# Row statistics of four tiles split between ScalarE and VectorE, an earlier weight column, convolutions queued later, and TensorE's first stage bound to its written sequence

## The chip, the core and the metric

The kernel runs on one core of a Trainium2 chip, as one launch. The metric is device time in microseconds (us) from the start to the end of the program. The profile comes from one further execution; its own time stands beside its span below.

## The reference, cut to what matters

One layer of a hybrid model works on 2048 latent rows of width 1024 (x) and 256 context rows (ctx).

```python
hc = modulate(rmsnorm(ctx, norm_mix), csh1, csc1)
logf_f, k_f, logf_b, k_b, vc = hgrn2_gates(hc @ w_in[:, :3 * w], ...)   # context: final scan states only
h = modulate(rmsnorm(x, norm_mix), sh1, sc1)
o, _, _ = token_mixers(h @ w_in, ..., hf_c, hb_c, ...)                  # 2 scans (4 heads) + gMLP unit (4 heads)
x = x + g1 * (o @ w_out)
h2 = modulate(rmsnorm(x, norm_ffn), sh2, sc2)
a, g = split(h2 @ w_up)                                                 # 2 x 2816 columns
x = x + g2 * ((a * gelu(conv3x3(g) + conv_b)) @ w_down)
return rmsnorm(x, norm_final)
```

`rmsnorm` divides a row by the root of the mean of its squares (plus a small constant). `token_mixers` runs a gated recurrence in both directions over 4 heads of 128 channels, started from the context's final states, and a gated unit that mixes positions in chunks of 128. `conv3x3` is a depthwise convolution over the 32 x 64 grid of latent rows. Everything is float32.

## The kernel before, in words

**Precision and TensorE.** A float32 product is made of three reduced-precision ones: each operand is split into a high part (a cast on ScalarE) and a low part (raw minus high, a subtraction on VectorE or GpSimd), and `mm3` issues high x high, high x low and low x high. All matmuls and transposes go through the class `Tensor` (L56 to L74), which also counts a planned time `t`. Profile rows name L70 for every matmul and L74 for every transpose, so products are told apart by their tiles: `pj` (input projection), `sc` and `mi` (scan, transposes), `dn` and `up` (later stages).

**Stage 1, the input projection and the scan (L183 to L1194).** x is done in two halves of 1024 rows, each transposed and modulated into `xh` and `xl` (8 blocks of 128 channels by 1024 rows). `run_banks` (L536) takes a list of banks: a column of 128 output channels and 512 rows (256 for context), so 24 matmuls a bank, followed by a sink that hands the result on. Before a bank it makes sure that the weights of this column and the next exist: `load_raw` (L209) issues a load on SP's queue, `split_w` (L216) casts on ScalarE and subtracts on VectorE, late for the next column in the steady state (there is then one raw buffer). Between the eighths of a 512-row bank `slot()` gives side work its turn: three pumps (`Pump`, L134) hold generators that write out a few instructions, then name the planned time after which they want the next turn. `need` (L647) steps a pump until something is done.

**Order.** `pin` (`keep_in_program_order`) puts an instruction behind the one traced before it on its engine. The program may move the others, by its own estimate of when operands are ready. Here the transposes of x in `x_first` (L414) and `x_second` (L451) are pinned, the other matmuls and transposes of the stage are not.

**Start of x.** Four tiles `xg` (L350) and then four tiles `xk` (L427) of 128 rows make the first half of x. `x_square` (L244) squares a tile on ScalarE with the row sum as a second output, `x_scale` (L249) makes the reciprocal root through `rstd` (L115, GpSimd) and scales the tiles on VectorE. `x_start` (L426) writes this out among the context's banks; the first bank of x needs `xg` transposed ("x0a"), the second needs `xk` ("x0b"). Their written order is the list in L1144, where `c` is a context bank. `ctx_state` (L618) makes a context head's states; `add_ctx(0)` is called ahead of the first bank of x.

**The second half of x.** It is prepared by `x_second`, parked in DRAM and loaded again after the first sequence of banks (L1150 to L1153: 16 loads, 8 for the first 512 rows, 8 for the rest). The second sequence (L1155) begins with the columns 0 and HW of the gate; the first run is told to prepare column 0 ahead (`peek`, L539), column HW is loaded by the second run. The scan of a head is `hg` (L783). The first half's reverse direction waits for states of the second and is finished by `deferred` (L887), whose results go through `o_out` (L742): squares on ScalarE, `rstd`, scaling to `on` on VectorE, and then transposes of `on` on TensorE, each a callback some planned us after the last. Ahead of the last four banks `wo_hook` calls `open_wo` (L1158), which steps all pumps until they are empty, so that buffers can be given over to the output projection.

**Output projection (L1353 to L1388).** 16 row tiles, each 48 matmuls into `dn`, then add x, square, and after each pair `second_norm` (L1295), which transposes and modulates for the next stage. For the last pair its first yield is 9.0. `fetch_x` (L1344) loads x's rows; the last tile shares a buffer with the weights of unit 1, the second of the units of the next stage, so that unit's second half loads only behind the eviction.

**Up-projection and convolution (L1586 to L1619).** A unit (L1231) makes 256 columns with seven products of 12 matmuls in place of eight (a Strassen scheme), for each half of the rows. `prep` (L1247) splits operands three products ahead: cast to `Ah` on ScalarE, subtraction to `Al` on GpSimd. After a gate unit's last product `after` (L1505) appends two convolutions to `work`; each (`conv`, L1431) is a first step on ScalarE and 8 taps on VectorE over 128 x 1024, then a Gelu on ScalarE. Two convolution steps are written out after each product. In the second half (`hh` = 1) the one grid row that straddles the halves (`edges`) gets three small taps on VectorE (L1444), its Gelu (L1459) and its product on GpSimd (L1460). `need` (L1478) steps convolutions until a result exists. Then comes the down-projection.

Of the kernel before, what the change touches and what calls it, by code (L numbers as in the profile page):

```python
# [18 lines left out]
P = 128  # L19
D = 1024  # L20
# [35 lines left out]
class Tensor:  # L56


    def __init__(self, engine):
        self.engine, self.t = engine, 0.0  # L60

    def matmul(self, out, lhsT, rhs, **kw):
        n = 1
        for _, count in rhs.ap[1:]:
            n *= count
        if lhsT.ap[1][1] < P and out.ap[0][1] == lhsT.ap[1][1]:
            self.t += 2 * (n / 1200 + 0.016) / 4
        else:
            self.t += n / 2400 + 0.0135 if rhs.dtype == F32R else 2 * max(0.112, n / 1200 + 0.005)
        return self.engine.matmul(out, lhsT, rhs, **kw)  # L70

    def transpose(self, out, in_, identity):
        self.t += 0.109
        return self.engine.transpose(out, in_, identity)  # L74
# [3 lines left out]
def tile_trunk(ctx, tc, x, c, cx, c_ctx, w_ada, b_ada, norm_mix, norm_ffn, w_in, hg_norm, sgu_g, sgu_b,  # L78
# [105 lines left out]
    with es1:  # L184
# [59 lines left out]
        def x_square(xs, ss, i0=0, keep=pin):  # L244
            for i, xt in enumerate(xs):
                jk = pm.tile([P, D], BF16, tag="acc", name="xjk")
                keep(S.activation(jk, xt, AF.Square, accum_out=ss[:, i0 + i:i0 + i + 1]))

        def x_scale(xs, ss, keep=pin):  # L249

            r = rstd(pm, ss[:, :len(xs)], len(xs), 1.0 / D, keep=keep)
            for i, xt in enumerate(xs):
                keep(V.tensor_scalar(out=xt, in0=xt, scalar1=r[:, i:i + 1], scalar2=None, op0=ALU.mult))
# [100 lines left out]
        with tc.manual_schedule():  # L354
# [55 lines left out]
            x_square(xg[:2], xss, keep=lambda i: i)  # L410
# [3 lines left out]
        def x_first(g0, xs):  # L414
            for k in range(NK):
                pt = bank("mi")
                for i in range(4):
                    pin(T.transpose(pt[:, i * P:(i + 1) * P], xs[i][:, k * P:(k + 1) * P], ident))
                sl = slice(g0 * P, g0 * P + 512)
                x_mod(pt, k, xh[:, k, sl], xl[:, k, sl], 512, S if k % 2 else V)  # L420
                if k % 2:
                    yield 1.6
# [3 lines left out]
        def x_start():  # L426
            xs = [key_tile(t, name="xk") for t in "MMMR"]  # L427
            ss = x_sums()
            x_square(xg[2:], ss)
            yield 1.0  # L430
# [105 lines left out]
        def run_banks(banks, peek=None):  # L536

            keys = [(b[0], b[2]) for b in banks]
            tail = [(peek, 512)] if peek is not None else []  # L539
            for i, (col, n0, n, sink, pre) in enumerate(banks):  # L540
# [4 lines left out]
                for key in up[:2]:  # L545
                    if key not in nxt:
                        nxt[key] = split_w(key, raws["w"] == [0] and key != up[0])
# [7 lines left out]
                for k in range(k0, NK):  # L555
                    if k and n == 512:
                        slot()
                        if k == 3:
                            split_low()
                        if k == 6 and len(up) > 2 and up[2] not in nxt and not w_raw:  # L560
                            load_raw(up[2])
                    w_products(pj[:, :n], (hi, lo), hiT, loT, sl, k, k + 1)
# [115 lines left out]
        ctx_banks = banks  # L678

# [459 lines left out]
        xa = [(xa[0][0], 0, 512, xa[0][3], lambda p=xa[0][4]: (need(bg_q, "x0a"), add_ctx(0), p())),  # L1139
# [9 lines left out]
        run_banks(seq, 0)  # L1149
        for q in range(0, TH, 512):  # L1150
            for k in range(0, NK, 2):
                ld(xh[:, k:k + 2, q:q + 512].bitcast(F32), xh_d[:, k:k + 2, q:q + 512])
                ld(xl[:, k:k + 2, q:q + 512].bitcast(F32), xl_d[:, k:k + 2, q:q + 512])  # L1153
# [40 lines left out]
        hg_q.flush()  # L1194

# [98 lines left out]
    with tc.tile_pool(name="po", bufs=1, reuse_waits="tile") as po:  # L1294
# [49 lines left out]
        def fetch_x(t):  # L1344
            xt = raw_tile2(2 if t == nt_ - 1 else 1 + 2 * (t % 2))
            ld(xt.rearrange("p a b -> p (a b)"), x[t * P:(t + 1) * P, :])
            return xt.rearrange("p a b -> p (a b)")
# [5 lines left out]
        for t, (hh, g) in enumerate(tiles):  # L1353
# [4 lines left out]
            if t + 1 < nt_:  # L1358
                ops[t + 1] = split_o(t + 1, raw_o.pop(t + 1))
                xts[t + 1] = fetch_x(t + 1)  # L1360
            if t + 2 == nt_:
                units[0].load()
            if t + 1 == nt_:
                units[1].load_half(0)
# [14 lines left out]
            if t + 1 == nt_:  # L1379
                units[1].load_half(1)  # L1380
            xs.append(xn)
            if g % 2:
                bg_q.drain()
                how = (ubank, 6.0, 3.0) if t + 1 < nt_ else (lambda: dbank()[:, 0, :], 9.0, 4.5)
# [35 lines left out]
    vals, work, tapped = {}, [], set()  # L1420
# [10 lines left out]
    def conv(hh, f, e):  # L1431
# [6 lines left out]
        for t in range(1, 9):  # L1438
            V.scalar_tensor_tensor(out=cr, in0=gt[:, t // 3:t // 3 + RH, t % 3:t % 3 + GW],  # L1439
                                   scalar=taps[:, t * NF + f:t * NF + f + 1], in1=cr, op0=ALU.mult, op1=ALU.add)  # L1440
            yield
        if hh:
            for t in range(6, 9):
                V.scalar_tensor_tensor(out=e[:, 0, :], in0=gt[:, 1, t % 3:t % 3 + GW],  # L1444
                                       scalar=taps[:, t * NF + f:t * NF + f + 1], in1=e[:, 0, :],
                                       op0=ALU.mult, op1=ALU.add)
# [10 lines left out]
        else:  # L1457
            pin(S.activation(vt[:, GW:], cp, AF.Gelu))
            S.activation(e[:, 0, :], e[:, 0, :], AF.Gelu)  # L1459
# [18 lines left out]
    def need(which, key):  # L1478

        while key not in which:  # L1480
            if not conv_step():
# [23 lines left out]
    def after(u, i, p):  # L1505
# [32 lines left out]
        if kind == "g" and i == 6:  # L1538
            for ff in (f, f + 1):
# [4 lines left out]
                work.append(conv(hh, ff, edge(hh, ff)))  # L1544
# [41 lines left out]
    for n, (u, i) in enumerate(prods):  # L1586
# [32 lines left out]
        conv_step() and conv_step()  # L1619
    assert not work  # L1620
# [250 lines left out]
```

## Time and profile before

| | |
|---|---|
| median of 3 runs | 2398.88 us (2397.96 to 2399.17) |
| profiled execution, its own time | 2401.17 us |
| its span in the trace | 2399.4 us |
| mean granted clock of TensorE | 0.995 |
| busy share: TensorE, VectorE, ScalarE, GpSimd | 98%, 71%, 41%, 33% |

Times in the trace count from the start of the span. A row of the timeline gives the start, the duration, the engine (PE is TensorE, DVE VectorE, ACT ScalarE, POOL GpSimd, SPq SP's queue of transfers), the line, and what is written from what; in brackets how long the engine had stood and what released it. Matmuls overlap in the pipeline, so their durations are longer than the distance of their starts. The granted clock (PEclk) is a share of TensorE's 2.4 GHz.

### The profile page before, as it was taken

How to read it: one execution, taken by the hardware profiler on the slowest of the kernel's cores; microseconds unless marked ns; L12 is line 12 of the kernel's file. 1: busy time of each engine (PE TensorE's matmuls, PEld its weight loads, DVE VectorE, ACT ScalarE, POOL GpSimd, SP SyncE). 2: the span in 40 equal slices, each digit the busy share in tenths (PEclk: the TensorE clock that was granted, in tenths of full speed). 3: DMA queues.
4: the chain of work that ended last, by engine and by line, in shares of the span. 5: the costliest groups of instructions: out<-in, count | busy, mean ns of one | idle time of the engine just before them, and what ended most of it. 6: DMA issues, size and time to landing. Idle time of an engine off the chain costs nothing.

```text
span 2399.4 us, 38721 instructions
## 1 busy us (share of the span) xinstructions
PE 2347.6 (98%) x14951; PEld 1935.9 (81%) x14951; DVE 1701.9 (71%) x2331; ACT 977.9 (41%) x1762; POOL 799.7 (33%) x741
## 2 busy tenths in 40 slices
PE   7999999999999999999999999999999999999998
PEld 5787887878887887887788888888788888888887
DVE  4655677556667653666898787689999984776876
ACT  4673443443445442544433333334333333232343
POOL 0010000000211111003787877878787860000011
PEclk9999999999999999999999999999999999999999
DMA  8454443574435536678522223642222259844744
GB/s 308 150 184 148 135 125 120 184 276 152 160 120 180 177 115 220 205 242 290 180 90 88 83 92 94 248 166 87 87 93 88 85 176 342 270 145 134 250 154 168
DMA packets 305428, 396.39 MB, mean 165 GB/s; under 512 B 33609, under 2 KB 216657, under 8 KB 302557
## 3 DMA queue, kind: packets, MB, share of 16 engines
q1 hardware_dynamic: 301956, 393.17, 49.4%
q8 instruction: 118, 1.93, 0.3%
q10 hardware_dynamic: 3289, 0.76, 0.1%
q14 instruction: 65, 0.53, 0.1%
HBM read 284.73 MB, written 109.13 MB: 164 GB/s over the span
## 4 chain that ended last, share of the span: by engine, by line
PE 50%; POOL 1%; DVE 1%; DMA 1%; issue 0%; SPq 0%; ACT 0%; POOLq 0%; ACTq 0%
PE up L70 32%; PE dn L70 17%; POOL Al L126 1%; DMA raw<-in_w_up_dram 0%; POOL raw L1265 0%; POOL cv L1534 0%; POOL fl L1261 0%; DMA m<-cv 0%; DVE dn L1439 0%; DMA sT<-wd 0%; DVE fl L126 0%; DVE fl L1314 0%; DMA gs<-gp 0%; SPq L1541 0%; DVE gp L1523 0%
## 5 line engine op out<-in xcount | busy, mean ns | idle before, releaser
L1439 DVE SCALAR_TENSOR_TENSOR dn<-gp,taps,dn 128x1024 f32<-128x1024 f32 x352 | 449.0, 1282 | 14.7 <-ACT dn L1436 11.6
L70 PE MATMUL up<-yfar,Ah 128*128 128x512 f32 x1232 | 394.5, 390 | 0.0
L70 PE MATMUL dn<-thl,mhl 128*128 128x512 f32 x1680 | 381.0, 389 | 0.0
L126 POOL TENSOR_TENSOR Al<-raw,Ah 128x512 fp32r<-128x512 f32 x264 | 343.9, 1314 | 79.0 <-ACT Ah L125 76.9
L70 PE MATMUL pj<-xh,whi 128*128 128x512 f32 x896 | 368.4, 411 | 0.0
L70 PEld LDWEIGHTS dn<-thl,mhl 128*128 128x128 f32 x1680 | 315.5, 188 | 65.4 <-issue 0.2
L70 PE MATMUL pj<-xh,wlo 128*128 128x512 f32 x896 | 351.1, 392 | 1.1 <-DVE wlo L225 1.1
L70 PE MATMUL pj<-xl,whi 128*128 128x512 f32 x896 | 350.8, 392 | 0.3 <-DVE xl L126 0.3
L125 ACT CAST Ah<-raw 128x512 fp32r<-128x512 f32 x264 | 162.4, 619 | 317.9 <-PE up L70 254.4
L70 PE MATMUL up<-xah,Al 128*128 128x512 f32 x704 | 275.5, 391 | 5.6 <-POOL Al L126 5.5
L70 PE MATMUL up<-xah,Ah 128*128 128x512 f32 x704 | 275.3, 391 | 1.2 <-ACT Ah L125 1.2
L70 PEld LDWEIGHTS up<-yfar,Ah 128*128 128x128 f32 x1232 | 231.6, 188 | 48.0
L70 PE MATMUL up<-xal,Ah 128*128 128x512 f32 x528 | 205.7, 390 | 0.0
L70 PE MATMUL up<-yfar,Al 128*128 128x512 f32 x528 | 205.5, 389 | 0.0
L70 PEld LDWEIGHTS pj<-xh,wlo 128*128 128x128 f32 x896 | 168.5, 188 | 38.4 <-DVE wlo L225 1.8
L70 PEld LDWEIGHTS pj<-xh,whi 128*128 128x128 f32 x896 | 169.1, 189 | 35.3 <-issue 3.5
L70 PEld LDWEIGHTS pj<-xl,whi 128*128 128x128 f32 x896 | 169.2, 189 | 29.1 <-DVE xl L126 0.6
L70 PE MATMUL dn<-wo,o 128*128 128x512 f32 x768 | 182.8, 394 | 0.8 <-DVE nt L732 0.8
L70 PEld LDWEIGHTS dn<-wo,o 128*128 128x128 f32 x768 | 142.1, 188 | 30.0 <-DVE nt L732 1.0
L70 PEld LDWEIGHTS up<-xah,Al 128*128 128x128 f32 x704 | 132.6, 188 | 35.0 <-POOL Al L126 7.6
L70 PEld LDWEIGHTS up<-xah,Ah 128*128 128x128 f32 x704 | 132.6, 188 | 29.2 <-ACT Ah L125 1.8
L222 ACT CAST whi<-raw 128x1024 fp32r<-128x1024 f32 x68 | 71.3, 1049 | 125.5 <-PE pj L70 102.2
(321 smaller groups left out, 3630.4 us busy)
## 6 DMA issues: line engine op xcount, KB each, us to landing
raw<-in_w_up_dram SPq DMA_DIRECT2D x88, 512.0 KB, 3.7
mr<-m SPq DMA_DIRECT2D x85, 512.0 KB, 5.1
raw<-in_w_in_dram SPq DMA_DIRECT2D x68, 512.0 KB, 4.1
sT<-wd SPq DMA_DIRECT2D x88, 256.0 KB, 4.9
raw<-in_w_ada_dram SPq DMA_DIRECT2D x32, 512.0 KB, 4.9
yfar<-yd SPq DMA_DIRECT2D x14, 1024.0 KB, 17.4
m<-cv SPq DMA_DIRECT2D x22, 544.0 KB, 2.8
raw<-in_w_down_dram SPq DMA_DIRECT2D x22, 512.0 KB, 4.1
```

Source lines behind the costliest of these rows:

```text
L70: return self.engine.matmul(out, lhsT, rhs, **kw)
L125: keep(S.copy(hi, raw))
L126: (eng or G).tensor_sub(lo, raw, hi.bitcast(F32))
L222: S.copy(hi, raw)
L1439: V.scalar_tensor_tensor(out=cr, in0=gt[:, t // 3:t // 3 + RH, t % 3:t % 3 + GW], scalar=taps[:, t * NF + f:t * NF + f + 1], in1=cr, op0=A ...
```

## The change

It has these parts, in the order of the diff:

- `Tensor` has a hook `keep` through which every matmul and transpose goes. From the first `run_banks` of stage 1 to the end of the stage it is `pin`, so TensorE runs the written sequence there.
- Rows of `xg[1]` and `xg[2]` get their mean square on VectorE (`x_stats`: two statistics calls over 512 columns, one that joins them, and two small GpSimd operations for mean squared plus variance) in place of a square on ScalarE. The remaining squares scale by 1/sqrt(1024) so that sums are means.
- `x_start` and `x_first` have other yields, context banks get one more `slot()` in their middle, and `ctx_state` of head 0 is queued one bank earlier.
- Column HW is loaded for the second sequence behind the first 8 loads of x's second half and ahead of the other 8, which are pinned. `peek` becomes a list, and a column in it is not split late.
- The last row tile of x gets a buffer of its own, so unit 1 is loaded whole at the last row tile; the last `second_norm` yields 10.5 first.
- New convolutions go to `fresh` and join `work` at the end of a product, behind that product's casts and steps.
- In the second half the edge's taps are written after tap 4 and its Gelu after tap 6, pinned, in place of after tap 8.

The diff, with the lines of the kernel before at each place:

```diff
@@ L59 @@
     def __init__(self, engine):
-        self.engine, self.t = engine, 0.0
+        self.engine, self.t, self.keep = engine, 0.0, lambda i: i
@@ L69 @@
             self.t += n / 2400 + 0.0135 if rhs.dtype == F32R else 2 * max(0.112, n / 1200 + 0.005)
-        return self.engine.matmul(out, lhsT, rhs, **kw)
+        return self.keep(self.engine.matmul(out, lhsT, rhs, **kw))
@@ L73 @@
         self.t += 0.109
-        return self.engine.transpose(out, in_, identity)
+        return self.keep(self.engine.transpose(out, in_, identity))
@@ L246 @@
                 jk = pm.tile([P, D], BF16, tag="acc", name="xjk")
-                keep(S.activation(jk, xt, AF.Square, accum_out=ss[:, i0 + i:i0 + i + 1]))
+                keep(S.activation(jk, xt, AF.Square, scale=D ** -0.5, accum_out=ss[:, i0 + i:i0 + i + 1]))
+
+        def x_stats(xt, s_, keep=pin):
+            bs = pm.tile([P, 4, 6], F32, tag="bs", name="xbs", bufs=2)
+            mv = pm.tile([P, 4, 2], F32, tag="mv", name="xmv", bufs=2)
+            for i in range(2):
+                keep(V.bn_stats(out=bs[:, i, :], in_=xt[:, i * 512:(i + 1) * 512]))
+            keep(V.bn_aggr(out=mv[:, 0, :], in_=bs[:, :2, :]))
+            keep(G.tensor_mul(s_, mv[:, 0, 0:1], mv[:, 0, 0:1]))
+            keep(G.tensor_add(s_, s_, mv[:, 0, 1:2]))
@@ L251 @@
-            r = rstd(pm, ss[:, :len(xs)], len(xs), 1.0 / D, keep=keep)
+            r = rstd(pm, ss[:, :len(xs)], len(xs), 1.0, keep=keep)
@@ L409 @@
             xss = x_sums()
-            x_square(xg[:2], xss, keep=lambda i: i)
+            x_square(xg[:1], xss, keep=lambda i: i)
+            x_stats(xg[1], xss[:, 1:2], keep=lambda i: i)
@@ L421 @@
                 if k % 2:
-                    yield 1.6
+                    yield 1.3
@@ L428 @@
             ss = x_sums()
-            x_square(xg[2:], ss)
-            yield 1.0
+            yield 0.0
+            yield 0.0
+            x_square(xg[3:], ss, 1)
+            x_stats(xg[2], ss[:, 0:1])
+            yield 2.0
@@ L536 @@
-        def run_banks(banks, peek=None):
+        def run_banks(banks, peek=()):
@@ L538 @@
             keys = [(b[0], b[2]) for b in banks]
-            tail = [(peek, 512)] if peek is not None else []
+            tail = [(col, 512) for col in peek]
@@ L546 @@
                     if key not in nxt:
-                        nxt[key] = split_w(key, raws["w"] == [0] and key != up[0])
+                        nxt[key] = split_w(key, raws["w"] == [0] and key != up[0] and key not in tail)
@@ L555 @@
                 for k in range(k0, NK):
+                    if k and (n == 512 or k == 4):
+                        slot()
                     if k and n == 512:
-                        slot()
@@ L678 @@
         ctx_banks = banks
+        ctx_banks[5] = (*banks[5][:4], lambda: add_ctx(0))
@@ L1138 @@
         xa = part(0, "g0")
-        xa = [(xa[0][0], 0, 512, xa[0][3], lambda p=xa[0][4]: (need(bg_q, "x0a"), add_ctx(0), p())),
+        xa = [(xa[0][0], 0, 512, xa[0][3], lambda p=xa[0][4]: (need(bg_q, "x0a"), p())),
@@ L1148 @@
         seq += rest
-        run_banks(seq, 0)
+        T.keep = pin
+        run_banks(seq, [0])
         for q in range(0, TH, 512):
+            if q:
+                load_raw((HW, 512))
             for k in range(0, NK, 2):
-                ld(xh[:, k:k + 2, q:q + 512].bitcast(F32), xh_d[:, k:k + 2, q:q + 512])
-                ld(xl[:, k:k + 2, q:q + 512].bitcast(F32), xl_d[:, k:k + 2, q:q + 512])
+                for t, d in ((xh, xh_d), (xl, xl_d)):
+                    i = ld(t[:, k:k + 2, q:q + 512].bitcast(F32), d[:, k:k + 2, q:q + 512])
+                    if q:
+                        pin(i)
@@ L1194 @@
         hg_q.flush()
+        T.keep = lambda i: i
@@ L1344 @@
         def fetch_x(t):
-            xt = raw_tile2(2 if t == nt_ - 1 else 1 + 2 * (t % 2))
-            ld(xt.rearrange("p a b -> p (a b)"), x[t * P:(t + 1) * P, :])
-            return xt.rearrange("p a b -> p (a b)")
+            if t == nt_ - 1:
+                xt = first_o[0]()[:, 0].bitcast(F32)
+            else:
+                xt = raw_tile2(1 + 2 * (t % 2))
+            xt = xt.rearrange("p a b -> p (a b)")
+            ld(xt, x[t * P:(t + 1) * P, :])
+            return xt
@@ L1359 @@
                 ops[t + 1] = split_o(t + 1, raw_o.pop(t + 1))
+            if t + 1 < nt_ - 1:
                 xts[t + 1] = fetch_x(t + 1)
+            elif t + 1 == nt_:
+                xts[t] = fetch_x(t)
@@ L1363 @@
             if t + 1 == nt_:
-                units[1].load_half(0)
+                units[1].load()
@@ L1378 @@
             S.activation(pd.rearrange("p a b -> p (a b)"), xn, AF.Square, accum_out=ss[:, g % 2:g % 2 + 1])
-            if t + 1 == nt_:
-                units[1].load_half(1)
@@ L1383 @@
                 bg_q.drain()
-                how = (ubank, 6.0, 3.0) if t + 1 < nt_ else (lambda: dbank()[:, 0, :], 9.0, 4.5)
+                how = (ubank, 6.0, 3.0) if t + 1 < nt_ else (lambda: dbank()[:, 0, :], 10.5, 4.5)
@@ L1420 @@
-    vals, work, tapped = {}, [], set()
+    vals, work, fresh, tapped = {}, [], [], set()
@@ L1440 @@
                                    scalar=taps[:, t * NF + f:t * NF + f + 1], in1=cr, op0=ALU.mult, op1=ALU.add)
+            if hh and t == 4:
+                for tt in range(6, 9):
+                    V.scalar_tensor_tensor(out=e[:, 0, :], in0=gt[:, 1, tt % 3:tt % 3 + GW],
+                                           scalar=taps[:, tt * NF + f:tt * NF + f + 1], in1=e[:, 0, :],
+                                           op0=ALU.mult, op1=ALU.add)
+            if hh and t == 6:
+                pin(S.activation(e[:, 0, :], e[:, 0, :], AF.Gelu))
             yield
-        if hh:
-            for t in range(6, 9):
-                V.scalar_tensor_tensor(out=e[:, 0, :], in0=gt[:, 1, t % 3:t % 3 + GW],
-                                       scalar=taps[:, t * NF + f:t * NF + f + 1], in1=e[:, 0, :],
-                                       op0=ALU.mult, op1=ALU.add)
@@ L1458 @@
             pin(S.activation(vt[:, GW:], cp, AF.Gelu))
-            S.activation(e[:, 0, :], e[:, 0, :], AF.Gelu)
@@ L1480 @@
         while key not in which:
+            if not work:
+                work.extend(fresh)
+                fresh.clear()
@@ L1543 @@
                     ld(gp[ff % 4][:, 0, 1:GW + 1], gs_d[ff][:, 0, :])
-                work.append(conv(hh, ff, edge(hh, ff)))
+                fresh.append(conv(hh, ff, edge(hh, ff)))
@@ L1619 @@
         conv_step() and conv_step()
+        work.extend(fresh)
+        fresh.clear()
```

## Rows read from the trace of the kernel before

**Rows 1.** The page's first part: busy us, share of the span and instructions of each engine.

```profile
PE 2347.6 (98%) x14951; PEld 1935.9 (81%) x14951; DVE 1701.9 (71%) x2331; ACT 977.9 (41%) x1762; POOL 799.7 (33%) x741
```

**Rows 2.** TensorE's waits by releaser, whole span: us in total, times, longest.

```profile
PE up L70 <- POOL Al L126: 5.5, 4, 3.0
...
PE mi L74 <- DVE on L752: 3.1, 3, 1.1
```

**Rows 3.** Timelines of TensorE and ScalarE at the start: start us, us, instruction, [idle before].

```profile
43.42 0.39 PE L70 MATMUL pj<-ch,whi 128*128 128x256 f32 x1 [2.08 <-ACT whi L222]
...
49.11 0.37 ACT L607 COPY vv<-pj 128x256 f32<-128x256 f32 x1 [3.21 <-PE pj L70]
...
64.92 1.07 ACT L247 ACTIVATE xjk<-xk 128x1024 bf16<-128x1024 f32 x1
```

**Rows 4.** VectorE's groups by shape: count, busy us, mean ns, idle before.

```profile
L715 DVE BATCH_NORM_STATS2 bs<-mi 128x6 f32<-128x128 f32 x64 | 16.3, 277 | 13.0 <-PE mi L74 12.9
```

**Rows 5.** Timelines of VectorE and TensorE, 69 to 74 us.

```profile
69.46 2.74 DVE L253 TENSOR_SCALAR xk<-xk,rs 128x1024 f32<-128x1024 f32 x4
...
70.42 0.27 PE L74 MATMUL mi<-ident,xk 128*128 128x128 f32 x1
```

**Rows 6.** Timeline of TensorE, 498 to 508 us.

```profile
498.00 0.40 PE L70 MATMUL pj<-xh,wlo 128*128 128x512 f32 x1
500.58 1.10 PE L70 MATMUL sc<-Q,K 128*32 128x64 f32 x64 [2.18 <-DVE Q L525]
503.72 3.65 PE L74 MATMUL mi<-ident,K 128*128 128x128 f32 x16 [2.04 <-DVE K L595]
```

**Rows 7.** SP's queue, its loads at L1153, VectorE and ScalarE, 487 to 511 us.

```profile
494.10 0.91 SPq L211 DMA_DIRECT2D raw<-in_w_in_dram  x1
...
DMA to landing us min/median/max: 6.3/8.4/10.6
...
487.65 1.22 DVE L225 TENSOR_TENSOR wlo<-raw,whi 128x1024 fp32r<-128x1024 f32 x1
...
509.59 1.05 ACT L222 CAST whi<-raw 128x1024 fp32r<-128x1024 f32 x1
```

**Rows 8.** Windows: stretch, busy us of each engine (instructions), PEclk, DMA share, GB/s.

```profile
503.00:510.00 7.00, 6.28 (x31) 6.31 (x32) 1.62 (x4) 3.89 (x8) 0.00 (x0) 0.52 0.57 196
900.00:914.00 14.00, 11.76 (x63) 9.58 (x63) 4.89 (x7) 4.59 (x19) 4.23 (x5) 1.00 0.52 163
1714.00:1722.00 8.00, 4.98 (x16) 3.73 (x15) 6.18 (x9) 4.00 (x6) 8.00 (x8) 0.79 0.21 79
```

**Rows 9.** Timeline of TensorE, 901 to 914 us.

```profile
901.55 0.48 PE L70 MATMUL pj<-xh,whi 128*128 128x512 f32 x1
...
905.73 0.39 PE L70 MATMUL pj<-xh,whi 128*128 128x512 f32 x1
907.23 0.63 PE L74 MATMUL mi<-ident,on 128*128 128x128 f32 x4 [1.11 <-DVE on L752]
...
908.50 0.47 PE L70 MATMUL pj<-xl,whi 128*128 128x512 f32 x1
...
911.58 0.39 PE L70 MATMUL pj<-xh,wlo 128*128 128x512 f32 x1
913.10 0.63 PE L74 MATMUL mi<-ident,on 128*128 128x128 f32 x4 [1.13 <-DVE on L752]
```

**Rows 10.** Timelines of TensorE and ScalarE, 1132 to 1168 us.

```profile
1133.01 0.55 PE L74 MATMUL dn<-ident,cv 128*128 128x128 f32 x3 [1.69 <-DVE cv L1299]
...
1167.42 0.50 PE L70 MATMUL up<-xah,Ah 128*128 128x512 f32 x1 [1.19 <-ACT Ah L125]
...
1163.12 1.21 ACT L1436 ACTIVATE dn<-gp,vec,taps 128x1024 f32<-128x1024 f32 x1 [3.16 <-DVE gp L1523]
```

**Rows 11.** Timeline of TensorE at 1718 us, and a row of ScalarE's waits.

```profile
1718.51 0.80 PE L70 MATMUL up<-xah,Al 128*128 128x512 f32 x1 [3.02 <-POOL Al L126]
...
ACT edges L1459 <- DVE edges L1444: 45.3, 20, 5.1
```

## The prediction

> **What bounds the kernel now.** I read the page first. TensorE is busy for 98% of the span and the next engine for 71% [rows 1], so only time in which TensorE stands, or runs at the lower of its two clock levels, can be won. The span of 2399.4 us less the 2347.6 busy leaves 52 us, part of them in the load phase and behind the last matmul, which the change leaves alone. Next came TensorE's waits by releaser: inside the stages no group is large, the first two of those that matter here come to 5.5 and 3.1 us [rows 2]. Then I read the timelines around each wait, to see what releases it and whether TensorE now runs other work in between, and the windows for the granted clock.
>
> One thing has to be read from code and trace together. TensorE's instructions do not run as written now: only transposes of x are pinned, and the program's ordering moved others past whatever it took to be late. Where a long wait would stand in the written sequence, the trace shows matmuls of a later bank between the two parts of a chain. Bound, these come behind the wait.
>
> **The change part by part.** Minus is time saved.
>
> *Start, 35 to 105 us.* A context bank waits 2.08 us for its weights, which ScalarE casts behind two squares. Moving xg[1] and xg[2] to VectorE takes two squares of 1.07 us off ScalarE, 2.1 us [rows 3]. A statistics call over 128 columns takes 0.28 us [rows 4]; the four calls over 512 are, by estimate, between 4 x 0.28 = 1.1 and 16 x 0.28 = 4.4 us, and I take 2.7, spread over two tiles, on an engine that waits for ScalarE there. Their small GpSimd operations are two more links of that chain. The scale factor on the square costs nothing: it is the same instruction. Against it stands the binding. ScalarE's squares of x's second half end at 65.99 us, after an idle stretch of 3.21 [rows 3]. VectorE scales those tiles until 72.20, and their transposes start one at a time at 70.42 [rows 5], with context matmuls between: TensorE has other work while they become ready. Bound, the first of them stands in the third eighth of the first gate bank of x, which TensorE reaches before they are ready. ScalarE, relieved by 2.1 us and perhaps half the 3.21, would end its squares at 62, and the 6.2 us from there to scaled tiles give 68, or 66 if VectorE has less in between. From there TensorE has five eighths of a bank of x, 15 x 0.23 = 3.4 us, and about 1 us of context bank still to do to be where it now is at 70.4. So it arrives between 70.4 and 72.4, less what later banks then no longer wait. I take 0. Ends: -4.2 (the 2.08 goes and ScalarE's 2.1 reaches TensorE whole) and +9 (tiles scaled at 72.2 as now, so 6.2 us late, and 2.8 of slow clock). ctx_state put one bank earlier, the second slot per context bank and the other yields only decide where these pieces stand; the operations are the same.
>
> *From the first sequence to the second.* At 498.23 us TensorE has no weights for column HW and runs the scan's scores, transposes and state products early, with waits of 2.18 and 2.04 us [rows 6]. The column's load is issued at 494.10, behind sixteen loads of x; the SP queue's loads of x land 6.3 to 10.6 us after issue, and the cast comes at 509.59 [rows 7]. Behind the waits the clock is granted at 0.52 from 503 to 510 [rows 8]; 0.48 of these 7 us, 3.3, is lost. So up to 4.2 + 3.3 = 7.5 us can go. In the new order the load stands behind eight loads of x. Its buffer is free when the subtraction for the column before is done, at 488.87 now [rows 7], sooner once that is no longer held back. Issued by 488.5 and landing after the median 8.4 us, it gives 496.9; cast 1.05 and subtraction 1.22 make 499.2, about 1 us late. The eight loads of x's second half now queue behind it, pinned, one load later; the bank that reads them starts a bank's 24 x 0.23 = 5.5 us after 498.2 and takes them pair by pair, so I charge nothing, and 3 us at the end of the range. I take -6.5; ends -7.5 and -1.
>
> *open_wo, 900 to 914 us.* This hook writes out all that is left of the scan ahead of the last four banks. Now 19 matmuls of the next bank run between the deferred product and the transposes of `on`, then 14 more before the second four, and still two waits of 1.11 and 1.13 us remain [rows 9]. Bound, the 33 matmuls come behind. The chain of add, squares, rstd and scaling takes 907.23 - 901.55 = 5.68 and 913.10 - 908.50 = 4.60 us, and TensorE stands for both. Cost: 33 x 0.227 = +7.5. The clock now stays at 1.00 from 900 to 914, with waits of 1.1, while waits of 2 us were followed by 0.52 [rows 8]; standing 10 us in 12 should bring the low level. A low stretch that falls on a wait is free, so I take +1.7, half of what 503 to 510 lost. The Trainium skill (TensorE: Matmul & The Clock Gate, Part 1) calls the low clock the default, which activity releases; by it the full 3.3 would be lost and the sum be 1.6 us worse. The two rows agree with it in direction. Together +9.2; ends +4 and +11.
>
> *Other bound places.* The third wait for `on`, 0.9 us by the difference of [rows 2] and [rows 9], may have a few matmuls moved ahead of it: +0.7 for three. Elsewhere +0.3. Ends 0 and +2.
>
> *Output projection to up-projection.* The last transposes wait 1.69 us for a scaled row tile; the first yield grows from 9.0 to 10.5, which puts 1.5 us of matmuls ahead: -1.5. x's last tile in its own buffer lets unit 1's second half load before the eviction. At 1167.42 an up product waits 1.19 us for a cast that ScalarE holds behind a convolution's first step, itself waiting 3.16 us for VectorE [rows 10]. Adding convolutions at the end of a product puts the casts ahead: -1.2. Together -2.7; ends 0 and -2.9.
>
> *Convolution of the second half.* TensorE's longest wait here, 3.02 us, is for a GpSimd subtraction whose cast came late; ScalarE lost 45.3 us in 20 waits to the edge's Gelu, up to 5.1 each [rows 11]. Edge products at tap 4 and the Gelu at tap 6 give VectorE two taps of lead. Behind the wait the clock of 1714 to 1722 is 0.79, 0.21 x 8 = 1.7 us [rows 8]. Of these 4.7 I take -3.5, and -0.5 of the remaining 2.5 us for GpSimd [rows 2]. Convolutions that start later may cost a wait elsewhere. Ends -6 and +2.
>
> Sum: 0 - 6.5 + 9.2 + 1.0 - 2.7 - 4.0 = -3.0 us. The profiled execution took 2401.17 us with a span of 2399.4, 1.8 around it, and lies 2.3 above the median of the runs, 2398.88. No term scales with that, so I subtract from the median: **2395.9 us**. A difference of 0.2%, 4.8 us, is about what a measurement of this kernel can tell from none.
>
> **Rivals.** *A, the waits go and the binding is cheap.* For: every wait that the change aims at has a releaser that it moves, and the clock held from 900 to 914. Start -4.2, boundary -7.5, open_wo +7.5, others +0.5, projection -2.9, convolution -4.7: -11.3, so 2387.6. Against: the start needs ScalarE's squares done some 6 us sooner.
>
> *B, slower: x's second half stops TensorE at the start.* If its tiles are scaled no earlier than now, TensorE stands bound in the first gate bank: start +9, the rest as forecast, +6.0, so 2404.9. It decides from a scaling that ends after about 71 us. For: ScalarE serves casts, squares and row tiles as before. Against: two squares fewer.
>
> *C, the convolution's wait moves on.* VectorE's taps and edge products stay as many, so a later product waits instead: projection -1.5, convolution 0, sum +2.2, so 2401.1.
>
> *D, the column's load is not early in fact.* Issued at 494.1 it lands at 502.5 and gives weights at 504.8; bound, TensorE stands 6.6 us for them, so only 1 of the 7.5 goes: sum +2.5, 2401.4.
>
> **How the numbers follow.** Forecast 0.36, A 0.30, B 0.18, C 0.12, D 0.04. A third of the forecast's chance lies beyond 0.2%, so faster is 0.30 + 0.12 = 0.42; same 0.24 + 0.12 + 0.04 = 0.40; slower 0.18. The range 2385.5 to 2404 takes in A down to 2 us below its value and leaves out most of B. As cases of both signs hold the chance, the forecast's own range stands beside it: 2391 to 2399.7.
>
> **What would show it.** Right: no wait and clock 1.00 from 498 to 510, and a load of column HW ahead of x's second half; two waits of about 5 us for `on` with no matmul of a later bank between; no wait of 3 us in the convolution; fewer and shorter waits of ScalarE for the edge. Wrong: a wait of over 4 us for the scaling of x's second half at the start (B); waits for `on` still near 1 us; a new wait for x's loads near 505.

## The result and the profile after

The changed kernel took 2408.61 us (median of 7 runs, 2405.14 to 2411.16) against 2398.88 us: 1.0036 times the time of before, 95% interval 1.0024 to 1.0047. It is slower by 0.36%, outside the forecast range and on the other side.

First the page of the changed kernel, to be read against [rows 1].

```profile
PE 2348.1 (98%) x14951; PEld 1937.3 (81%) x14951; DVE 1703.8 (71%) x2337; ACT 976.1 (41%) x1758; POOL 801.5 (33%) x745
```

TensorE's waits by releaser in the changed kernel, against [rows 2] (us in total, times, longest):

```profile
PE mi L74 <- DVE on L767: 10.7, 3, 5.4
PE mi L70 <- ACT ckt L646: 4.2, 2, 2.7
PE pj L70 <- ACT whi L222: 3.3, 1, 3.3
PE up L70 <- POOL Al L126: 2.6, 2, 1.8
...
PE pj L70 <- ACT ch L342: 2.1, 1, 2.1
PE up L70 <- DVE cv L1561: 2.0, 1, 2.0
...
PE mi L74 <- ACT kt L858: 1.8, 2, 1.3
```

Shares of busy time tell nothing here: they are the same as before. The list of waits does: `on` went from 3.1 to 10.7 us, and `ckt`, `whi`, `ch` (the context's operand), `kt` and `cv` are new or longer.

To see where time was lost and won I took the starts of the same matmuls in each trace: of the second transfer of modulation weights ("load"), of the 1057th, 1441st, 2497th and 2688th 512-row matmul of the input projection, and of the last matmul. Each column is the time between two such marks, in us; at each of the marks every kernel has run the same TensorE instructions. `before_again` and `again` are second executions of the two kernels.

```
kernel          load  start  boundary  middle  last four banks  the rest
before          11.6  388.1     128.6   336.1             65.2    1462.2
before_again    10.2  387.0     128.3   334.2             65.2    1462.4
changed          9.7  395.9     121.6   334.6             76.1    1458.0
again           11.0  395.2     122.1   334.4             76.1    1458.5
```

By the means of two: load -0.6, start +8.0, boundary -6.6, middle -0.7, last four banks +10.9, the rest -4.1; together +7.0. The medians differ by 9.7 (the first seven runs) and 7.8 us (the runs of `again`); the traces account for 7.0.

**Start.** Timeline of TensorE in the changed kernel, to be read against [rows 3, 5].

```profile
36.87 0.58 PE L70 MATMUL pj<-ch,whi 128*128 128x256 f32 x1 [2.08 <-ACT ch L342]
...
61.09 0.28 PE L70 MATMUL pj<-ch,wlo 128*128 128x256 f32 x1
64.64 0.50 PE L70 MATMUL pj<-xh,whi 128*128 128x512 f32 x1 [3.27 <-ACT whi L222]
...
67.42 0.63 PE L70 MATMUL pj<-xh,whi 128*128 128x512 f32 x1
67.85 0.63 PE L70 MATMUL pj<-xl,whi 128*128 128x512 f32 x1
...
68.70 1.55 PE L74 MATMUL mi<-ident,xk 128*128 128x128 f32 x8
...
77.69 1.16 PE L70 MATMUL mi<-cb,ckt 128*128 128x128 f32 x8 [1.54 <-ACT ckt L646]
...
144.81 2.07 PE L70 MATMUL mi<-cb,ckt 128*128 128x128 f32 x8 [2.68 <-ACT ckt L646]
```

The wait of 2.08 us at 43 us is gone, but one of the same length has come at 36.87 us, and TensorE stands 3.27 us ahead of x's first gate bank. Its matmuls then follow each other by 0.43 us in place of 0.23. ScalarE's timeline shows what the cast of that bank's weights (at 63.55) stood behind:

```profile
55.02 1.05 ACT L247 ACTIVATE xjk<-xk 128x1024 bf16<-128x1024 f32 x1
...
57.01 1.05 ACT L247 ACTIVATE xjk<-xk 128x1024 bf16<-128x1024 f32 x1
...
60.01 1.05 ACT L247 ACTIVATE xjk<-xk 128x1024 bf16<-128x1024 f32 x1
...
61.33 1.04 ACT L247 ACTIVATE xjk<-xk 128x1024 bf16<-128x1024 f32 x1
...
63.55 1.04 ACT L222 CAST whi<-raw 128x1024 fp32r<-128x1024 f32 x1
```

ScalarE has no idle stretch from 53.2 to 66 us, and the cast of the gate bank's weights stands behind the four squares of `xk`. These are scaled in time: their transposes at 68.70 hardly wait. The other new waits of the start are for ScalarE too: `ch`, `ckt`, and 1.25 us for `kt` at 278.85 us.

**Boundary and last four banks.** SP's queue and ScalarE at the boundary, against [rows 7]:

```profile
494.14 0.46 SPq L1171 DMA_DIRECT2D xl<-xl_d  x1
494.69 0.42 SPq L211 DMA_DIRECT2D raw<-in_w_in_dram  x1
495.16 0.57 SPq L1171 DMA_DIRECT2D xh<-xh_d  x1
...
501.73 1.05 ACT L222 CAST whi<-raw 128x1024 fp32r<-128x1024 f32 x1
```

The load of column HW stands between the two halves of x's loads, its cast comes 7.9 us earlier in a trace that runs some 6 us later, and no wait is left. TensorE and VectorE at `open_wo`, against [rows 9]:

```profile
898.04 1.05 PE L70 MATMUL mi<-bs,Qb 128*128 128x128 f32 x8
904.52 1.09 PE L74 MATMUL mi<-ident,on 128*128 128x128 f32 x4 [5.42 <-DVE on L767]
905.40 1.92 PE L70 MATMUL mi<-bs,Qb 128*128 128x128 f32 x8
911.65 0.66 PE L74 MATMUL mi<-ident,on 128*128 128x128 f32 x2 [4.34 <-DVE on L767]
...
900.23 0.68 DVE L920 TENSOR_TENSOR op<-mi,op 128x512 f32<-128x512 f32 x1
903.68 0.69 DVE L767 TENSOR_TENSOR on<-op,rs 128x512 f32<-128x512 f32 x1 [2.76 <-POOL rs L120]
```

No matmul of the next bank stands between the product and the transposes, so TensorE waits for the whole chain. Windows of the changed kernel, columns as in [rows 8]:

```profile
61.00:70.00 9.00, 5.20 (x21) 3.82 (x20) 7.61 (x16) 5.33 (x11) 1.20 (x2) 0.81 0.27 78
503.00:510.00 7.00, 7.00 (x121) 5.61 (x111) 7.00 (x9) 4.71 (x10) 2.20 (x1) 1.00 1.05 403
900.00:915.00 15.00, 6.14 (x22) 5.42 (x23) 4.49 (x7) 2.55 (x16) 3.84 (x5) 0.59 0.39 123
1665.00:1680.00 15.00, 13.04 (x51) 10.27 (x50) 15.00 (x17) 3.22 (x6) 12.89 (x11) 0.89 0.20 73
1714.00:1722.00 8.00, 8.00 (x37) 6.64 (x36) 8.00 (x10) 2.45 (x4) 7.92 (x8) 1.00 0.35 132
```

The clock went the way of the waits: 0.52 became 1.00 at the boundary and 0.79 became 1.00 at 1714 us in the convolution, while it fell to 0.81 at the start, 0.59 at `open_wo` and 0.89 at a new stop at 1670 us, all three 1.00 before.

**Convolution.** The stop of 3.02 us [rows 11] is gone, and ScalarE's waits for the edge fell from 45.3 to 16.6 us; at 1670 us there is a new stop. Timelines of TensorE, VectorE and GpSimd in the changed kernel:

```profile
1670.09 0.74 PE L70 MATMUL up<-yfar,Ah 128*128 128x512 f32 x2 [1.97 <-DVE cv L1561]
...
1662.25 0.28 DVE L1469 SCALAR_TENSOR_TENSOR edges<-gp,taps,edges 128x64 f32<-128x64 f32 x1
...
1665.56 1.40 DVE L1469 SCALAR_TENSOR_TENSOR edges<-gp,taps,edges 128x64 f32<-128x64 f32 x1
...
1669.26 0.68 DVE L1561 TENSOR_TENSOR cv<-up,cv 128x512 f32<-128x512 f32 x1
...
1665.58 1.30 POOL L1282 TENSOR_TENSOR s<-raw 128x512 f32<-128x512 f32 x1
```

The row of ScalarE's waits:

```profile
ACT edges L1473 <- DVE edges L1469: 16.6, 6, 3.5
```

VectorE has no idle time from 1665 to 1680 us, and the edge products (`edges`) now stand ahead of the product that TensorE waits for (`cv`, at 1669.26).

### The profile page after: what moved, and what is told of

The parts are those of the page before. It is cut to its first block, busy times and chain, and to the rows that moved or that the text cites. A ratio compares the mean times of both kernels' runs of the same rounds, so it can differ in the third digit from the quotient of the medians.

```text
span 2403.4 us, 38735 instructions
## 1 busy us (share of the span) xinstructions
PE 2348.1 (98%) x14951; PEld 1937.3 (81%) x14951; DVE 1703.8 (71%) x2337; ACT 976.1 (41%) x1758; POOL 801.5 (33%) x745
## 4 chain that ended last, share of the span: by engine, by line
PE 83%; DVE 6%; issue 4%; POOL 2%; DMA 2%; ACT 2%; SPq 0%; POOLq 0%; DVEq 0%; ACTq 0%
PE up L70 29%; PE dn L70 25%; PE pj L70 22%; PE mi L70 3%; DVE dn L1465 2%; PE mi L74 2%; PE sc L70 2%; DMA wa<-in_w_ada_dram 1%; DVE Q L538 1%; POOL rs L120 1%; PE up L74 1%; POOL Al L126 1%; DVE edges L1469 0%; DVE K L615 0%; POOL rs L118 0%
```

## The experiments

The standing theory: the loss is the binding, at two places (the start, and the last four banks); the other parts bring what the boundary, projection and convolution columns show. Rivals: the new order of the start loses by itself; the early column gains only because TensorE is bound.

**again** and **before_again**: the two kernels once more, no edit.

> The changed kernel once more, for a second trace and more times. Its profiled execution lay 4.0 us above the profiled one of before, its median 9.7 us above the median of before; the difference of 5.7 us is open. Theory (the bound order passes on what varies at the start): median 2405 to 2411, and where a second trace is longer than the first, the extra time has come about before 200 us. Rival (the variation is the clock behind the stops at 900 us, or lies in the convolution): the traces agree to 1 us up to 850 us.

> The kernel before once more, for a second trace. Its first profiled execution lay 2.3 us above the median of its runs. Theory: a trace near the median differs from the first one at the start (weights of the modulation land earlier) and at single waits in the convolution, each under 2 us. Rival: it differs by the clock, in one stretch of low clock more or less.

`again`: 2406.73 us (1.003, 1.0019 to 1.0042). Its trace is 1.6 us longer than the first, 1.1 of it ahead of 65 us; up to 850 us the two stay within 1.3. That is too little to decide between theory and rival. `before_again` (2396.58) says more: 4.6 us shorter than the first trace, 2.5 of that gone by 57 us (1.4 in the load column), 1.2 in the scan between 645 and 680 us, the rest in small steps; the mean clock is 0.995 in both. So the first trace of before was a long one through its load phase and single waits, and a difference of two single traces is good to some 5 us only.

**unbound**: everything but the binding.

```diff
-        T.keep = pin
         run_banks(seq, [0])
```

> All of the change but the binding of TensorE. Theory (the binding loses 5.8 us at the start and 10.9 at the last four banks, the early column gives 7.0, the output projection 2.7 and the convolution 1.5 without it): about 2388 (2385 to 2392), waits for the scaled o near 1.1 us as before, boundary at 498 us still without a wait. Rival 1 (the start is lost by what its row statistics and yields do, not by the binding): 2394. Rival 2 (the early column gains only because TensorE is bound): 2395.

2388.18 us (0.9956, 0.9943 to 0.9968): faster than both kernels by the amount expected. The column still has no wait, so rival 2 falls; rival 1's 2394 is out too, though part of its mechanism comes back below. TensorE's waits in this kernel:

```profile
PE pj L70 <- ACT whi L222: 5.2, 2, 5.0
...
PE mi L74 <- DVE on L767: 3.1, 3, 1.1
...
PE mi L70 <- ACT ckt L646: 0.8, 1, 0.8
```

The wait for the weight cast is longer here (5.0 against 3.3 us), and yet the start column is 390.1, 5.5 less than bound. It is not that other work was moved ahead of this stop: TensorE has run the same 291 instructions when it comes to it in both kernels. It comes to it 0.9 us earlier, having lost less on the way (`ch` 0.6 against 2.1), and leaves it 0.8 us later. Most of the 5.5 us is won behind it, where the second stop for `ckt` is 0.8 in place of 2.68 us and the one for `kt` is gone. A listed wait is not the loss; the distance between marks is.

**wo_free** and **start_free**: bound at one of the two places only.

```diff
@@ wo_free: in wo_hook @@
+            T.keep = lambda i: i
             open_wo()
@@ start_free: T.keep = pin moved from the first run_banks into pre_g @@
                     raws["w"] = [0]
+                    T.keep = pin
```

> The change, with TensorE unbound from the hook ahead of the last four banks on. Theory: the two waits for the scaled o go back from 5.4 and 4.6 us to about 1.1 each, 10.9 us less than the changed kernel: 2397.7 (2395 to 2400). Rival (the chain of squares, root and scaling is late itself, the order costs only 7.5): 2401.

> The change, with TensorE bound only from the first gate bank of the first sequence on (about 170 us). Theory (the binding costs 5.8 us at the start, and the spread of the runs comes from there): 2397 to 2403. Rival (the order in which ScalarE serves squares and the weight cast costs the 5.8, bound or not): 2408, and a wait of some 3 us for a weight cast at about 61 us stays.

wo_free: 2397.08 us (0.9991, 0.9982 to 1.0); the last four banks take 65.1 as before, and the waits for `on` are 3.2 in all. start_free: 2400.68 us (1.0008, 0.9999 to 1.0017); start 390.9. Both theories hold, the one for the start as a sum over its whole column. The rival of start_free is right in that the long wait for the cast stays (5.0 us), and wrong in its price.

**bind_only**: the kernel before with the binding and nothing else.

> The kernel before with nothing but the binding of TensorE. Theory: the last four banks lose 10.9 us, the boundary at 498 us stands for a late column in place of filling in (6.6 less the 4.2 it waits now, and the clock kept: about +1), the start waits for tiles scaled at 72 us: +6 to +9. Sum 2417 to 2420. Rival (the new start is what makes the bound start slow): 2411.

2422.35 us (1.0099, 1.0085 to 1.0113), above the theory. Start 395.8 and last four banks 76.2 are as in the changed kernel. Alone, the binding costs 8.2 and 11 us there; in the start its price depends on the rest of the change, 5.5 us where the new start is in. The boundary was misjudged: +6.3 where +1 was expected. TensorE's waits:

```profile
PE mi L74 <- DVE on L752: 10.6, 3, 5.4
PE pj L70 <- ACT whi L222: 9.7, 1, 9.7
PE mi L74 <- DVE xk L253: 7.3, 11, 3.5
```

Here the column's load is issued at 502.34 us behind all sixteen loads, and bound TensorE stands 9.7 us for it: rival D's mechanism, which the early load forestalls in the changed kernel (no run separates the load's new place from the earlier split of column 0). And the start's longest stop is for `xk`, rival B's place, while `ckt` is 0.7: its 4.2 us need the new start as well as the binding.

**late_sq** and **late_sq_bound**: unbound and bound, with the squares of `xk` one step later, so that the weight cast stands ahead of them.

```diff
-                if i in (1, 2):
-                    x_square(xs[2 * i - 2:2 * i], ss2, 2 * i - 2)
+                if i in (2, 3):
+                    x_square(xs[2 * i - 4:2 * i - 2], ss2, 2 * i - 4)
```

> The change without the binding, and the squares of the fifth to eighth row tile written one step later, so that ScalarE casts the weights of x's first gate bank ahead of them. Theory (those squares hold the cast back: with and without binding TensorE waits 3 to 5 us for it, and runs some 9 matmuls at the low clock behind): the wait goes below 2 us and 2 to 4 us are won against the change without binding: 2384 to 2386.5. Rival (the tiles that are squared later stop TensorE by as much): 2388 with a new wait for the scaled tiles of 3 us or more.

> The changed kernel, bound, with the squares of the fifth to eighth row tile written one step later, so that the cast for x's first gate bank stands ahead of them on ScalarE. Theory (bound, TensorE has nothing else to run until those tiles are scaled, so the stop moves from the weights to them): the wait of 3.3 us for the cast goes, waits for the scaled tiles of 2 to 4 us come, 2404 to 2407. Rival (the order of the cast alone costs what the start lost): 2401 to 2403.

late_sq: 2386.99 us (0.9952, 0.994 to 0.9965), just above the theory's band and 1.2 below unbound, which the spread of the runs (2384.64 to 2389.27) does not separate. In its trace the wait for the cast is down to 0.2, the clock stays at 1.00 from 61 to 70 us (0.62 unbound), and the start column is 386.4, 3.7 less.

late_sq_bound: 2410.38 us (1.0051, 1.0038 to 1.0063), no better than the changed kernel, and higher than both expected. TensorE's waits:

```profile
PE mi L70 <- ACT ckt L646: 4.2, 2, 2.7
PE mi L74 <- DVE xk L262: 3.3, 6, 1.7
...
PE pj L70 <- ACT whi L222: 1.9, 1, 1.9
```

Part of the stop moved from the cast (1.9 us left of 3.3) to the scaled tiles, and the start column stays at 396.2. The same edit wins 3.7 us unbound and nothing bound.

**old_start**, **no_stats** and **late_sq_sq**: the start's other parts. old_start is unbound with the start as before; no_stats is the changed kernel, late_sq_sq is late_sq, both with the squares of `xg[1]` and `xg[2]` back on ScalarE:

```diff
-            x_square(xg[:1], xss, keep=lambda i: i)
-            x_stats(xg[1], xss[:, 1:2], keep=lambda i: i)
+            x_square(xg[:2], xss, keep=lambda i: i)
...
-            x_square(xg[3:], ss, 1)
-            x_stats(xg[2], ss[:, 0:1])
+            x_square(xg[2:], ss)
```

> The change without the binding and with the whole start as it was before (squares on ScalarE, yields, one slot for a context bank, states of head 0 queued where they were). Theory (the new start wins as much at the first weights as it loses at the cast behind the squares): 2388 (2386.5 to 2389.5), the wait of 5 us for a weight cast is gone, one of 2.1 us at 43 us is back. Rival 1 (statistics on VectorE are a gain of 2 us that shows once nothing is bound): 2390.5. Rival 2 (the new start is a loss by itself): 2383 to 2385.

> The changed kernel, bound, with all four squares of the first tiles on ScalarE as before. Theory (ScalarE sets the start): its chain is two squares longer, about 2.1 us, and the stop at the first gate bank of x comes to 4 to 5.5 us: 2409 to 2411. Rival (the statistics and their small GpSimd operations lengthen the chain): 2405 to 2407.

> The unbound change with the later squares and without statistics on VectorE (all four squares of the first tiles on ScalarE). Theory (with the weight cast ahead of the later squares, ScalarE's time no longer sets the start, so two squares more cost under 1 us): 2386 to 2388. Rival (two squares of 1.07 us on ScalarE reach TensorE): 2389, with a wait of about 2 us for a weight cast near 43 us.

old_start: 2389.4 us (0.9961, 0.9948 to 0.9975), start 388.2, within the theory's band; the two waits for casts are 2.8 us in all, the longest 1.9. no_stats: 2406.78 us (1.0036, 1.0023 to 1.0048), which is the rival's number, though its start column is the longest of all, 398.4, 2 to 3 us over the changed kernel's, as the theory has it; the rest of that run was shorter (1456.7). Not settled. late_sq_sq: 2386.91 us (0.9948, 0.9936 to 0.9961), start 387.2 against 386.4. So the statistics on VectorE bring 2 to 3 us bound and 0.8 unbound by the start columns of single traces, and nothing by the medians.

One more mark divides the start: the 49th 512-row matmul, at 81 to 90 us, ahead of which every kernel has run 409 TensorE instructions (the same ones but for one). In us from the load mark:

```
kernel                            to the 49th   on to the 1057th
before, before_again              72.2, 71.0    315.9, 316.0
old_start (unbound)                     72.3           315.9
unbound                                 77.3           312.8
late_sq (unbound)                       73.3           313.1
bind_only                               79.1           316.7
changed, again                    78.2, 78.0    317.6, 317.2
late_sq_bound                           78.3           317.9
```

Two things fill the same time up to the 49th matmul, and each is enough: the new start's cast behind the squares (5.7 us unbound; all but 1.7 of it goes in late_sq), and the binding (7.5 us with the old start, 5.0 with the later squares). Together they cost 6.6. Two traces of one kernel differ by up to 1.2 here. Behind that mark the new start wins 3.2 us unbound and loses 1.4 bound.

**edge_only**, **fresh_only** and **edge_spread**: the convolution, all on late_sq. edge_only appends to `work` at once, fresh_only has the edge's taps and Gelu after tap 8 as before, edge_spread is this:

```diff
-            if hh and t == 4:
-                for tt in range(6, 9):
+            if hh and t in (3, 4, 5):
+                tt = t + 3
```

> The unbound change with the later squares, without the later queueing of convolutions (they join the list at once, as before). Theory (the new stop of 2.0 us at about 1650 us, for a product on VectorE, comes from the three edge products written after tap 4, the stop of 3.0 us at 1710 us went by them, and the stop of 1.9 us at about 1165 us comes from the later queueing): 1650 stays, 1710 stays gone, 1165 is that of before (1.4): within 1 us of 2387. Rival (the later queueing causes the 2.0): the stop at 1650 is gone, 2385.

> The unbound change with the later squares, with the edge's products and Gelu after tap 8 as before, the later queueing kept. Theory: the 2.0 us at 1650 go, the stop of about 3 us at 1710 and its slow clock are back (4.6 in all), so 2389 to 2390. Rival (the later queueing is what removed the stop at 1710): 2385.

> The unbound change with the later squares, and one edge product written after each of taps 3, 4 and 5 in place of three after tap 4. Theory (the stop of 2.0 us at about 1650 us comes from the sum of three products, 0.3 to 1.4 us each, on a VectorE that has no idle time there, not from their place): the stop stays at 1.5 to 2.0 us, the median within 1 us of 2387. Rival (three products in one step hold back the eviction behind them): the stop falls below 0.7 us and 1.3 us or more are won.

By medians the three are late_sq's equals: 2386.88 (0.9952, 0.9939 to 0.9966), 2386.26 (0.9954, 0.9942 to 0.9967) and 2386.11 us (0.9953, 0.9937 to 0.9968). The single stops tell more. Of TensorE's waits, first fresh_only, then edge_only, then edge_spread:

```profile
PE up L70 <- POOL Al L126: 6.1, 3, 2.7
```

```profile
PE up L70 <- POOL Al L126: 3.2, 2, 1.8
...
PE up L70 <- DVE cv L1559: 1.9, 1, 1.9
```

```profile
PE up L70 <- DVE cv L1560: 0.9, 1, 0.9
```

With the edge after tap 8, the stop of 2.7 us for `Al` is back and the one for `cv` is gone; with the early edge it is the other way round. That is the theory. The stop for `Al` at about 1165 us is 1.8 in edge_only as in late_sq, against the expectation of 1.4: later queueing does not make it. Nor is it what removed the wait of 1.19 us for a cast there [rows 10], which is gone in edge_only too; no trace shows what later queueing brings. Spreading the three products halves the `cv` stop: place and total both count, and neither theory nor rival has it whole.

## Why the prediction was wrong

**Start: forecast 0, found +8.0.** This step failed, and it decided the sign. I asked one question, whether `xk` would be scaled by the time TensorE gets to it, and answered it nearly right: scaling began at 66.36 and ended at 69.1 us, where I had put 66 to 68. But a bound TensorE stands for everything that ScalarE serves late, and I had checked only one thing. It stood 3.3 us for a weight cast behind the squares, 2.1 us for the context's operand (`ch`, the same in every kernel with a bound start and at most 0.6 in the others), 4.2 us for two copies of context states (`ckt`, 0.8 unbound) and 1.3 us for `kt`, and the clock fell. The cast behind the squares, at nothing in my sum, is a loss without the binding too: 5.7 us up to the 49th matmul, of which the new start wins 3.2 back later. With TensorE bound, late_sq_bound shows that repairing the cast hands the stop to the next operand: the start column is 395.2 to 398.4 bound in every form, 386.1 to 390.9 unbound. Rival B had the sign, nearly the time and the price (+9), but by luck: its sign was a scaling that ends after 71 us, and its place, the scaled tiles, is where bind_only and late_sq_bound stand, not the changed kernel. The squares' 2.1 us, my gain for ScalarE, were worth 2 to 3 us bound and 0.8 unbound by single traces, and nothing by the medians.

**Boundary: -6.5, found -6.6.** Right, and unbound keeps it (121.7 us). The load's issue was not at 488.5 but at 494.69, in a trace that runs some 6 us later.

**open_wo: +9.2, found +10.9.** Mechanism and place were right (wo_free gives all of it back); the clock term was mis-sized. The waits grew from 1.11 and 1.13 to 5.42 and 4.34, 7.5 us, as forecast. That leaves 3.4, by difference, for the clock in place of 1.7: between 912.96 and 915.95 us the next bank's matmuls follow by 0.43 us, and the small products between the waits took 1.92 in place of 1.05 us. The Trainium skill (TensorE: Matmul & The Clock Gate, Part 1) calls the low clock the default; the trace agrees with it, since 3.4 is near the full 3.3 that the forecast gave as the price by that rule.

**Other bound places: +1.0, found -0.7** over the middle, where the two traces of before differ by 1.9; no more can be said.

**Projection -2.7 and convolution -4.0, found -4.1 together.** The projection's share was right as a sum (-2.7 and -2.6 in two pairs of traces) and in part by luck: the wait for the scaled tile went, but where the wait of 1.19 us for a cast went, one of 1.8 us for `Al` came, and the later queueing, to which I gave 1.2, is not shown to bring anything. The convolution gave -1.5 and -1.8: the stop and its slow clock went, but I had put nothing on the products that the edge now places ahead of an eviction. Their new stop was followed by a clock of 0.89 over 15 us in the first trace (1.97 us) and by no slow clock in `again` (1.88 us). Rival C (the wait moves on) is half true.

With start +8, the forecast's own sum would have been +5.0, and with the clock and the convolution as found +9.3; the other bound places take 1.7 of it back.

## What to carry to other kernels

Binding an engine to its written sequence turns every late operand into a stop; ask of all operands in the bound stretch who serves them and when, not of the one that the change is about. Two causes that fill the same time do not add up: taking away one of them alone can show nothing, as the later squares did while TensorE was bound. If an early load is the aim, place the load and leave the consumer free: without the binding the rest of the change is 0.44% faster than before (late_sq and its variants 0.46 to 0.52%). Judge a stage by the distance between the same instructions in two traces, since a listed wait can grow while the stage gets shorter.

## What the hardware showed

The same product over 64 columns on VectorE took 0.28 us with GpSimd idle and 1.40 us where a GpSimd subtraction of 1.30 us began beside it; both ended within 0.1 us, at 1666.9 us. The Trainium skill (SBUF — State Buffer, section SBUF: two separate sides) says that VectorE, when both inputs of its instruction lie in SBUF (the on-chip memory), and GpSimd share a pair of ports that one of them holds for a whole instruction; these rows agree with it, and no run here isolates it. A tap over 1024 columns, which has one input in TensorE's output buffers (`dn`), took 1.28 us with GpSimd idle (at 1661.07 us) and with GpSimd busy (at 1664.37 us) alike.

A statistics call on VectorE took 0.28 us over 128 columns [rows 4] and 0.68 us over 512: the four of the changed start took 2.6 us, where the forecast estimated 2.7.

Two executions of one unchanged kernel differed by 4.6 us, over half of it before the 60th microsecond.
